# Sum of ReLU over rows: the last two rows closed on two engines, a store moved behind the loads, and the first pieces divided anew

## The chip, the cores and the metric

One core of one Trainium2 chip. The metric is the device time of one execution in microseconds (us). Each run also lists the span that its profile covers; the time is longer than the span, in the kernel before by 1.36 us on average.

## The reference

```python
x: [32, 512, 1024] float32
relu_x = np.maximum(x, 0)
return np.sum(relu_x, axis=-1).astype(np.float32)      # [32, 512]
```

16,384 rows of 1,024 numbers, 67.1 MB in, 64 KB out. The kernel puts 128 rows on the 128 partitions at a time, so there are 128 "rows" per partition.

## The kernel before

The first seven pieces are 16 rows each, in three buffers that take turns. For six of them ScalarE takes the ReLU in a few steps and VectorE sums rows behind it; `ACT_STEPS` and `DVE_STEPS` say how many rows a step has. From the seventh piece on each engine takes whole rows, ReLU and sum in one operation. The end comes in ever smaller loads (8, 4, 2, 1 rows), and the very last row in three parts.

```python
ACT_STEPS = [[7, 9], [7, 9], [4, 5, 7], [4, 5, 7], [4, 5, 7], [3, 4, 5]]
DVE_STEPS = [[7, 9], [7, 4, 5], [4, 5, 7], [4, 5, 7], [4, 5, 7], [3, 4, 5]]
TAIL = [8, 4, 2, 1]
LAST = [512, 224, 288]
# ... cut ...
    parts = [buf[:, tb, r, 0:n0], buf[:, tb, r, n0:n1], last[:, 0 : LAST[2]]]
    for k, (lo, hi) in enumerate([(0, n0), (n0, n1), (n1, D)]):
        sp.dma_start(out=parts[k], in_=xv[-1][:, BIG - 1, lo:hi]).then_inc(
            s_in[NBIG + len(TAIL) + k] if k < 2 else s_part, 16
        )
    sp.wait_ge(s_fact, 1)
    sp.wait_ge(s_fdve, 1)
    sp.dma_start(out=ov[1][:, :], in_=res[:, start[1] : start[2]]).then_inc(s_store, 16)   # bulk store
    sp.wait_ge(s_turn, 1)
    sp.dma_start(out=of[0:P].rearrange(...), in_=turned[0:P:32, 0:32]).then_inc(s_store, 16)
# ... cut: the row before the last is halved, its halves added ...
    n = LAST[2]
    act.wait_ge(s_in[-2], 16)
    on_act(parts[0], last[:, n : n + 1]).then_inc(s_part, 1)
    dve.wait_ge(s_in[-1], 16)
    on_dve(parts[1], last[:, n + 1 : n + 2]).then_inc(s_part, 1)
    dve.wait_ge(s_part, 16 + 2)
    on_dve(last[:, :], res[:, J - 1 : J]).then_inc(s_tdve, 1)      # 288 columns and two partial sums
    sp.wait_ge(s_tdve, 1)
    sp.dma_start(out=ov[-1][:, :], in_=res[:, start[-1] : J]).then_inc(s_out, 16)          # final store
    sp.wait_ge(s_store, 16 * (len(REGIONS) - 1))
    sp.wait_ge(s_out, 16)
```

The last load and the two partial sums lie side by side in `last`, so one operation closes the row (ReLU doesn't change the partial sums, which are never negative).

## Time and profile before

| what | value |
|---|---|
| time, median | 161.09 us (160.91 to 161.38, 3 runs) |
| span of the profiled run | 160.0 us (that run: 161.31 us) |
| DMA share, 9 to 120 us | 1.00, at 433 GB/s |
| VectorE, ScalarE busy | 76%, 63% |
| last load landed | 157.98 us |
| final store issued | 158.49 us |

The DMA stream is full from the start almost to the end (DMA share 0.93 in the first 9 us, 1.00 from there to 120 us, and 1.00 again as the mean of 120 to 150 us). So one reads only the two ends: from the landing of the last loads to the last store. The lines are in the prediction.

### The profile page before, as it was taken

What the parts mean: (1) busy time and instruction counts of PE and PEld (TensorE: products, weight loads), DVE (VectorE), ACT (ScalarE), POOL (GpSimd) and SP (SyncE); (2) the same over time, 40 slices, a digit from 0 to 9 for tenths busy, and PEclk for the clock granted to TensorE, in tenths of its full rate; (3) what the DMA queues carried; (4) which work ended last, traced back from release to release, by engine and by line L of the source; (5) the groups of instructions that cost most, each with busy time, mean ns of one, the idle gap of its engine ahead of it and who ended that gap; (6) DMA issues with size and microseconds to landing.
All of it is one profiled execution on the core that took longest, in us unless ns stands there. A gap on an engine that the chain in (4) does not pass through costs nothing.

```text
span 160.0 us, 150 instructions
## 1 busy us (share of the span) xinstructions
DVE 121.6 (76%) x59; ACT 101.4 (63%) x55; POOL 0.2 (0%) x4
## 2 busy tenths in 40 slices
DVE  0000000999959999999979989699899999598994
ACT  3000059990799708996099942999339980596973
POOL 0000000000000000000000000000000000000000
DMA  9997996996996997997998979969969969999993
GB/s 377 492 399 338 492 524 262 524 524 262 524 508 279 524 475 311 524 442 344 524 410 377 524 344 443 524 295 492 524 295 492 524 262 524 393 393 406 418 387 119
DMA packets 2457, 67.18 MB, mean 420 GB/s; under 512 B 536, under 2 KB 792, under 8 KB 1176
## 3 DMA queue, kind: packets, MB, share of 16 engines
q1 hardware_dynamic: 2456, 67.18, 97.8%
q14 instruction: 1, 0.01, 0.0%
HBM read 67.11 MB, written 0.07 MB: 420 GB/s over the span
## 4 chain that ended last, share of the span: by engine, by line
DMA 68%; ACT 18%; DVE 11%; SPq 1%; issue 0%
DMA buf<-in_x_dram 68%; ACT buf L137 18%; DVE res L152 11%; ACT buf L119 1%; SPq L98 1%; DVE last L122 0%
## 5 line engine op out<-in xcount | busy, mean ns | idle before, releaser
L152 DVE TENSOR_REDUCE res<-buf 128x7 f32<-128x7168 f32 (+4 forms) x17 | 100.1, 5920 | 33.6 <-ACT buf L137 33.6
L137 ACT ACTIVATE buf<-buf 128x7168 f32<-128x7168 f32 (+4 forms) x16 | 80.7, 5099 | 45.9 <-DMA buf<-in_x_dram 45.9
L119 ACT ACTIVATE buf<-buf 128x1024 f32<-128x1024 f32 (+1 forms) x19 | 19.0, 1001 | 9.2 <-DMA buf<-in_x_dram 9.2
L122 DVE TENSOR_SCALAR_CACHE_REDUCE buf<-buf 128x1024 f32<-128x1024 f32 (+2 forms) x19 | 20.8, 1144 | 2.9 <-DMA buf<-in_x_dram 2.7
L119 ACT ACTIVATION_READ_ACCUMULATOR buf<-buf 128x1 f32 x19 | 3.6, 187 | 0.0
L137 ACT ACT_TABLE_LOAD x1 | 1.3, 1283 | 1.3 <-PEq L215 1.3
L122 DVE DVE_READ_ACCUMULATOR buf<-buf 128x1 f32 x19 | 1.6, 82 | 0.0
L122 DVE TENSOR_SCALAR_CACHE_REDUCE last<-last 128x290 f32<-128x290 f32 x1 | 0.5, 455 | 0.2 <-ACT buf L119 0.2
L161 DVE STREAM_TRANSPOSE turned<-res 128x32 f32<-128x32 f32 x1 | 0.2, 211 | 0.0
L185 DVE TENSOR_TENSOR res<-half 128x1 f32<-128x1 f32 x1 | 0.2, 160 | 0.1
L215 POOL MEMSET const-bfloat16-1.0<- 128x1 bf16 x1 | 0.1, 101 | 0.0
L215 POOL MEMSET const-uint8-127<- 128x1 uint8 x1 | 0.1, 101 | 0.0
L215 POOL MEMSET const-float32-0.0<- 128x1 f32 x1 | 0.1, 98 | 0.2 <-issue 0.2
L215 POOL MEMSET const-float32-1.0<- 128x1 f32 x1 | 0.1, 98 | 0.0
L122 DVE DVE_READ_ACCUMULATOR last<-last 128x1 f32 x1 | 0.1, 82 | 0.0
## 6 DMA issues: line engine op xcount, KB each, us to landing
buf<-in_x_dram SPq DMA_DIRECT2D x1, 7680.0 KB, 21.3
buf<-in_x_dram SPq DMA_DIRECT2D x1, 4096.0 KB, 26.7
buf<-in_x_dram SPq DMA_DIRECT2D x1, 2048.0 KB, 31.2
buf<-in_x_dram SPq DMA_DIRECT2D x2, 512.0 KB, 18.8
buf<-in_x_dram SPq DMA_DIRECT2D x1, 1024.0 KB, 33.2
buf<-in_x_dram SPq DMA_DIRECT2D x1, 256.0 KB, 34.4
last<-in_x_dram SPq DMA_DIRECT2D x1, 144.0 KB, 34.3
buf<-in_x_dram SPq DMA_DIRECT2D x1, 112.0 KB, 34.1
```

Of the source, the lines that this page charges most:

```text
L98: sp.dma_start(out=buf[:, tb, r : r + n, :], in_=xv[-1][:, r : r + n, :]).then_inc(s_in[NBIG + i], 16)
L119: return act.activation(t, t, AF.Relu, accum_out=acc)
L122: return dve.tensor_scalar(out=t, in0=t, scalar1=0.0, scalar2=None, op0=ALU.max, op1=ALU.add, accum_out=acc)
L137: act.activation(t, t, AF.Relu).then_inc(s_act, 1)
L152: dve.tensor_reduce(out=res[:, c * BIG + r : c * BIG + r + n], in_=buf[:, c % NB, r : r + n, :], axis=X, op=ALU.add,).then_inc(s_dve, 1)
L161: dve.transpose(out=turned[:, :], in_=res[:, 0:32]).then_inc(s_turn, 1)
L185: dve.tensor_tensor(out=res[:, j0 + r : j0 + r + 1], in0=half[:, 0:1], in1=half[:, 1:2], op=ALU.add)
L215: nc = _bacc.Bacc("TRN2", target_bir_lowering=False, num_devices=1)
```

## The change

Its intent: the last piece becomes a run that crosses the border of the last two rows (112 columns of one, 256 of the other). ScalarE closes the one row and VectorE the other, at the same time. The bulk store of 111 columns of results goes out only when the next to last load has landed; the small store of `turned`, which stood behind it, now goes first. The division of the first pieces is changed as well.

```diff
-ACT_STEPS = [[7, 9], [7, 9], [4, 5, 7], [4, 5, 7], [4, 5, 7], [3, 4, 5]]
-DVE_STEPS = [[7, 9], [7, 4, 5], [4, 5, 7], [4, 5, 7], [4, 5, 7], [3, 4, 5]]
-TAIL = [8, 4, 2, 1]
-LAST = [512, 224, 288]
+ACT_STEPS = [[16], [7, 9], [7, 9], [7, 9], [4, 5, 7], [3, 4, 5]]
+DVE_STEPS = [[4, 5, 7], [7, 4, 5], [7, 4, 5], [7, 4, 5], [4, 5, 7], [3, 4, 5]]
+TAIL = [8, 4, 2]
+CUT = 912
+HEAD = 256
 ... cut ...
+    first, second, third = [(0, CUT), (D + D // 2, 2 * D), (D + HEAD, D + D // 2)]
+    for k, (lo, hi) in enumerate((first, second, third)):
+        sp.dma_start(out=flat[:, lo:hi], in_=rows[:, lo:hi]).then_inc(s_in[NBIG + len(TAIL) + k], 16)
+    sp.dma_start(out=seam[:, 2 : 2 + w + HEAD], in_=rows[:, CUT : D + HEAD]).then_inc(s_seam, 16)
+    ... store of `turned` ...
     sp.wait_ge(s_fact, 1)
     sp.wait_ge(s_fdve, 1)
+    sp.wait_ge(s_in[-1], 16)
     sp.dma_start(out=ov[1][:, :], in_=res[:, start[1] : start[2]]).then_inc(s_store, 16)
 ... cut ...
+    on_act(flat[:, lo : CUT // 2], seam[:, 0:1]).then_inc(s_half, 1)
+    on_dve(flat[:, CUT // 2 : hi], seam[:, 1:2]).then_inc(s_half, 1)
+    ... ScalarE sums `second` (512 columns), VectorE `third` (256) into seam[:, k + HEAD :] ...
+    act.wait_ge(s_seam, 16 + 2)
+    act.wait_ge(s_half, 2)
+    on_act(seam[:, 0:k], res[:, J - 2 : J - 1]).then_inc(s_last, 1)
+    dve.wait_ge(s_seam, 16 + 2)
+    on_dve(seam[:, k : k + HEAD + 2], res[:, J - 1 : J]).then_inc(s_last, 1)
```

More of the change, by code (lines that the diff above doesn't have):

```diff
@@ L36, in bass_relu_sum_kernel @@
     NBIG = len(CHUNKS)
-    assert BIG * NBIG + sum(TAIL) + 1 == J == sum(REGIONS) and sum(LAST) == D
+    assert BIG * NBIG + sum(TAIL) + 2 == J == sum(REGIONS)
     xr = x.rearrange("b s d -> (b s) d")
@@ L48, in bass_relu_sum_kernel @@
     buf = nc.alloc_sbuf_tensor("buf", [P, NB, BIG, D], fp32)
-    last = nc.alloc_sbuf_tensor("last", [P, LAST[2] + 2], fp32)
-    half = nc.alloc_sbuf_tensor("half", [P, 2], fp32)
+    w = D - CUT
+    seam = nc.alloc_sbuf_tensor("seam", [P, 2 + w + HEAD + 2], fp32)
     res = nc.alloc_sbuf_tensor("res", [P, J], fp32)
     turned = nc.alloc_sbuf_tensor("turned", [P, 32], fp32)
-    n_in = NBIG + len(TAIL) + len(LAST) - 1
+    n_in = NBIG + len(TAIL) + 3
     s_in = [nc.alloc_semaphore(f"s_in{i}") for i in range(n_in)]
@@ L60, in bass_relu_sum_kernel @@
     s_half = nc.alloc_semaphore("s_half")
-    s_part = nc.alloc_semaphore("s_part")
-    s_tdve = nc.alloc_semaphore("s_tdve")
+    s_seam = nc.alloc_semaphore("s_seam")
+    s_last = nc.alloc_semaphore("s_last")
     s_turn = nc.alloc_semaphore("s_turn")
@@ L102, in bass_relu_sum_kernel @@
         r += n
-    n0, n1 = LAST[0], LAST[0] + LAST[1]
-    parts = [buf[:, tb, r, 0:n0], buf[:, tb, r, n0:n1], last[:, 0 : LAST[2]]]
-    for k, (lo, hi) in enumerate([(0, n0), (n0, n1), (n1, D)]):
-        sp.dma_start(out=parts[k], in_=xv[-1][:, BIG - 1, lo:hi]).then_inc(
-            s_in[NBIG + len(TAIL) + k] if k < 2 else s_part, 16
-        )
-    sp.wait_ge(s_fact, 1)
-    sp.wait_ge(s_fdve, 1)
-    sp.dma_start(out=ov[1][:, :], in_=res[:, start[1] : start[2]]).then_inc(s_store, 16)
+    rows = xv[-1].rearrange("p j d -> p (j d)")[:, r * D : (r + 2) * D]
+    flat = buf[:, tb, r : r + 2, :].rearrange("p j d -> p (j d)")
+    first, second, third = [(0, CUT), (D + D // 2, 2 * D), (D + HEAD, D + D // 2)]
+    for k, (lo, hi) in enumerate((first, second, third)):
+        sp.dma_start(out=flat[:, lo:hi], in_=rows[:, lo:hi]).then_inc(
+            s_in[NBIG + len(TAIL) + k], 16
+        )
+    sp.dma_start(out=seam[:, 2 : 2 + w + HEAD], in_=rows[:, CUT : D + HEAD]).then_inc(s_seam, 16)
     sp.wait_ge(s_turn, 1)
@@ L115, in bass_relu_sum_kernel @@
     ).then_inc(s_store, 16)
+    sp.wait_ge(s_fact, 1)
+    sp.wait_ge(s_fdve, 1)
+    sp.wait_ge(s_in[-1], 16)
+    sp.dma_start(out=ov[1][:, :], in_=res[:, start[1] : start[2]]).then_inc(s_store, 16)
     def on_act(t, acc):
@@ L171, in bass_relu_sum_kernel @@
                 ins.then_inc(s_fact if i % 2 else s_fdve, 1)
-    for r, n, s in tail[:-1]:
+    for r, n, s in tail:
         act.wait_ge(s, 16)
@@ L177, in bass_relu_sum_kernel @@
             f(buf[:, tb, i, :], res[:, j0 + i : j0 + i + 1])
-    r, _, s = tail[-1]
-    act.wait_ge(s, 16)
-    dve.wait_ge(s, 16)
-    on_act(buf[:, tb, r, 0 : D // 2], half[:, 0:1]).then_inc(s_half, 1)
-    on_dve(buf[:, tb, r, D // 2 : D], half[:, 1:2]).then_inc(s_half, 1)
-    dve.wait_ge(s_half, 2)
-    dve.tensor_tensor(
-        out=res[:, j0 + r : j0 + r + 1], in0=half[:, 0:1], in1=half[:, 1:2], op=ALU.add
-    )
-    n = LAST[2]
+    lo, hi = first
+    act.wait_ge(s_in[-3], 16)
+    dve.wait_ge(s_in[-3], 16)
+    on_act(flat[:, lo : CUT // 2], seam[:, 0:1]).then_inc(s_half, 1)
+    on_dve(flat[:, CUT // 2 : hi], seam[:, 1:2]).then_inc(s_half, 1)
+    k = 2 + w
+    lo, hi = second
     act.wait_ge(s_in[-2], 16)
-    on_act(parts[0], last[:, n : n + 1]).then_inc(s_part, 1)
+    on_act(flat[:, lo:hi], seam[:, k + HEAD : k + HEAD + 1]).then_inc(s_seam, 1)
+    lo, hi = third
     dve.wait_ge(s_in[-1], 16)
-    on_dve(parts[1], last[:, n + 1 : n + 2]).then_inc(s_part, 1)
-    dve.wait_ge(s_part, 16 + 2)
-    on_dve(last[:, :], res[:, J - 1 : J]).then_inc(s_tdve, 1)
-    sp.wait_ge(s_tdve, 1)
+    on_dve(flat[:, lo:hi], seam[:, k + HEAD + 1 : k + HEAD + 2]).then_inc(s_seam, 1)
+    act.wait_ge(s_seam, 16 + 2)
[3 more added lines that the diff above has]
+    on_dve(seam[:, k : k + HEAD + 2], res[:, J - 1 : J]).then_inc(s_last, 1)
+    sp.wait_ge(s_last, 2)
     sp.dma_start(out=ov[-1][:, :], in_=res[:, start[-1] : J]).then_inc(s_out, 16)
```

## The prediction

> **What bounds the kernel now.** I read the page first (shares per engine, then the slices of the DMA row), then the transfer rate in a long stretch, then the chain that ended last, then the instructions of the last four microseconds, and at the end the packets of two short windows.
>
> ```profile
> DVE 121.6 (76%) x59; ACT 101.4 (63%) x55; POOL 0.2 (0%) x4
> ...
> DMA  9997996996996997997998979969969969999993
> ```
>
> ```profile
> 9.00:120.00 111.00, 86.32 (x15) 71.51 (x14) 0.00 (x0) 1.00 1.00 433
> ```
>
> The second fence is one stretch, 9 to 120 us: length, busy DVE, ACT and POOL, clock, DMA share, GB/s. The reader is to see that no engine is full while the transfers are: share 1.00 at 433 GB/s over 111 us. The starts of ScalarE's work on the big pieces in the timeline (41.10, 60.46, 79.80, 99.16, 118.52) are 19.35 us apart, and a piece is 8.39 MB, so 433.5 GB/s. The 67.1 MB need 154.8 us at that rate, out of a span of 160.0. What a change of this kind can touch is therefore only the rest: the start, up to the first bytes, and the end, from the last load to the last store. The end is this:
>
> ```profile
> 122.21 34.19 DMA buf<-in_x_dram
> 156.40 0.02 issue
> 156.42 1.56 ACT buf L119 x4
> 157.98 0.02 issue
> 158.00 0.46 DVE last L122 x2
> ```
>
> ```profile
> 156.95 0.19 ACT L119 ACTIVATION_READ_ACCUMULATOR buf<-buf 128x1 f32 x1
> 157.03 0.08 DVE L122 DVE_READ_ACCUMULATOR buf<-buf 128x1 f32 x1
> 157.08 0.63 ACT L119 ACTIVATE buf<-buf 128x512 f32<-128x512 f32 x1
> 157.17 0.16 DVE L185 TENSOR_TENSOR res<-half 128x1 f32<-128x1 f32 x1
> 157.37 0.39 DVE L122 TENSOR_SCALAR_CACHE_REDUCE buf<-buf 128x224 f32<-128x224 f32 x1
> 157.61 0.19 ACT L119 ACTIVATION_READ_ACCUMULATOR buf<-buf 128x1 f32 x1
> 157.68 0.08 DVE L122 DVE_READ_ACCUMULATOR buf<-buf 128x1 f32 x1
> 158.00 0.46 DVE L122 TENSOR_SCALAR_CACHE_REDUCE last<-last 128x290 f32<-128x290 f32 x1 [0.24 <-ACT buf L119]
> 158.38 0.08 DVE L122 DVE_READ_ACCUMULATOR last<-last 128x1 f32 x1
> 158.49 0.34 SPq L199 DMA_DIRECT2D out_dram<-res  x1
> ```
>
> Columns: start us, length us, engine, line, operation. The chain says that VectorE's closing reduce waited for ScalarE. I don't believe that name. ScalarE's accumulator read ends at 157.80 and VectorE starts at 158.00; where VectorE really waits for ScalarE (157.14 to 157.17, the addition of the halves) the gap is 0.03 us. The same reduce also waits for the last load:
>
> ```profile
> 123.69 0.44 SPq L106 DMA_DIRECT2D last<-in_x_dram  x1
> ```
>
> and the view of that tile gives 34.3 us from its issue to its landing, so 157.99. The last landing is what ends last, and ScalarE follows it by 0.2 us. After it come 0.46 us of VectorE and about 1.5 us of final store (issue at 158.49, landing 1.4 us later).
>
> [...]it is issued at 147.17, yet its small packets are not there then and come with the last loads, where nearly all packets under 512 B lie (these counts also hold a few packets of the completions). First 147.0 to 148.5, then 156.8 to 157.6:
>
> ```profile
> DMA packets 44, 0.64 MB, mean 426 GB/s; under 512 B 5, under 2 KB 5, under 8 KB 5
> ```
> ```profile
> DMA packets 240, 0.14 MB, mean 170 GB/s; under 512 B 170, under 2 KB 240, under 8 KB 240
> ```
>
> [...]the store's runs are 444 B (111 x 4). [...]the trace shows the second as an 82 ns read on VectorE and a 187 ns read on ScalarE.
>
> **The change part by part.**
> 1. *First pieces.* ScalarE takes piece 0 in one step of 16 rows. From 7,168 to 9,216 elements it goes from 6.17 to 7.87 us, 0.83 ns each, so 16,384 need 13.8 us: 21.75 + 13.8 = 35.6, where VectorE now starts (27.96 before). A piece in steps of 4, 5 and 7 costs VectorE 17.30 us (65.07 to 82.37), and the new order leaves it no wait between pieces: it finishes pieces 0 to 4 at 52.9, 70.2, 87.7 (with 0.2 of transpose), 105.0 and 122.3. These release the loads of pieces 3 to 6 and the tail. The loads ahead of them end at 60.4, 79.8, 99.1, 118.5 and 137.9. The smallest margin is 7.5 us: no bubble, 0 us. Piece 5 costs two rows alone (2.28) and 13.07: done at 137.65, just before piece 6 lands at 137.87, with another 0.5 us of VectorE idle time before the next landing. 0 us.
> 2. *Bytes of the end.* The last two rows were loads of 1024, 512, 224 and 288 columns and are now 912, 512, 256 and 368: same 2,048 columns, same four packets per partition. Last byte unmoved. The first load is 448 B per partition shorter: it lands some 0.13 us earlier, 156.27. The second lands near 156.90, the third, 32 columns more than before, near 157.24.
> 3. *ScalarE.* 1045 ns for 1,024 columns and 630 for 512 give 0.81 ns a column: 456 take 0.585, 156.27 to 156.86. It waits for the second load, runs 512 columns from 156.92 and has read its sum by 157.64 (before: 157.80).
> 4. *VectorE.* 685 ns for 512 and 386 for 224 give 1.04 ns a column: 456 take 0.63, done by 156.95; 256 take 0.42 from the third landing, sum read by 157.70. The addition (0.16 us) goes; it was hidden beside ScalarE.
> 5. *Closing.* Both engines now wait for the last load and for each other, then ScalarE closes 114 columns (0.31, with its read 0.41 us) while VectorE closes 258 (0.42, with its read 0.45 to 0.49; before 0.46 for 290). VectorE still ends last, 0.03 us sooner than before for its fewer columns.
> 6. *Bulk store late.* It now waits for the third load, so it is issued near 157.26, for 0.35 us, over long before the closing. From the final store (issue 158.49, first bytes seen in the window from 159.2 on) I estimate its packets at about 158.1, after all loads, and its landing near 158.9, before the final store's near 159.7. Nothing waits for it. What it gives is that the last load's stragglers no longer share the engines' final half microsecond with 128 packets of 444 B. Other loads of the end landed about 0.35 us after their last bytes (rate falls to nothing around 157.36, landing 157.99 is 0.6 after): if the store caused this excess, the landing comes about 0.25 earlier, 157.73.
>
> Sum: with the landing at 157.73 both engines are ready at 157.70, the closing ends near 158.22 instead of 158.46: 0.24 us gained. With the landing unmoved: 0.0 to 0.03. Weighted evenly and rounded up a little, since such a variant would hardly be kept for nothing: 0.2 us off 161.09, **160.87 us**.
>
> **The rivals.**
> (a) *The last landing is late for its own reasons.* For it: [...]the byte count is unchanged. Then the kernel stays at 161.05 to 161.1 and the chain names the load openly. Against: the earlier loads land with less lag.
> (b) *A new wait replaces the old.* Two engines must both finish and each needs the other's partial sum; a late ScalarE would hold VectorE too. It would need ScalarE over 0.1 us later than in step 3; its second load would have to land after 157.0. Time 161.1 to 161.2.
> (c) *The stream is starved early.* VectorE releases buffers up to 7.4 us later than before. Against: margins of 7.5 us and more. If wrong, several us, 163 or so; improbable.
> (d) *The late store delays the end*, being the last to land or holding the issuing queue. Against: 0.7 us of margin by the estimate in step 6. If wrong, 161.3.
>
> **Range and chances.** The runs before spread by 0.47 us (160.91 to 161.38), more than the effect. Two thirds for a gain of 0.1 to 0.4, a quarter for nothing, the rest for a small loss: 160.45 to 161.25. Over 2% would be 3.2 us; the whole end after the last load is about 2.7 us, so it can't be gained there: 0.005. Slower by that much needs (c): 0.005.
>
> **What would show it.** Step 1: VectorE without gaps from 35.6 to about 137.6, DMA share at 1.00 in the middle, pieces landing every 19.35 us. Steps 3 and 4: partial sums at about 157.65 and 157.70. Step 5: both closings start together, within 0.05 us of the last landing. Step 6: packets under 512 B gone from 156.8 to 157.6 save for completions, last landing near 157.7. The prediction is wrong if the DMA rate dips in the middle, if the closings start at 158.0 again, or if the final wait ends on the bulk store.

Its sum comes to 0.2 us off, 160.87 us; that the store causes the late landing, on which its 0.24 us case rests, was the author's assumption. The stream counts as full by the DMA share of 1.00 in its second fence. The store that "is issued at 147.17" is the bulk store. In the trace of the kernel before, its 128 packets of 444 B, 25 ns each, run from 156.84 to 157.54, and the 128 packets of the last load from 156.46 to 157.36. Which of the 16 engines carry them was not shown. The "completions" are packets of 4 B: the trace has 277 of them, as many as there are semaphore increments by DMA. The "second" of 82 and 187 ns is the read of the accumulator, a line of its own behind each reduce in the timeline.

## The result, and the profile after

The changed kernel takes 160.81 us median (160.72 to 161.02, 6 runs), the kernel before 161.06 us (160.91 to 161.38, 6 runs). The ratio is 0.9985, with a 95% interval of 0.9972 to 0.9998. A ratio is the mean time of one kernel's fast runs over that of the other's in the same rounds, so it isn't quite the ratio of these medians. By the limit of 2% the two are the same; the small gain is just clear of noise, and it came again in a second set (160.81 against 160.97, ratio 0.9983, interval 0.9969 to 0.9998).

The stretch from 9 to 120 us of the changed kernel, in the columns of the prediction's fence:

```profile
9.00:120.00 111.00, 84.47 (x16) 71.38 (x11) 0.00 (x0) 1.00 1.00 433
```

The stream is untouched: same share, same rate. The chain that ended last, in order of time (start us, length us, what):

```profile
35.50 34.59 DVE res L160 x6
...
124.39 32.60 DMA buf<-in_x_dram
156.99 0.02 issue
157.01 0.44 DVE buf L130 x2
157.45 0.02 issue
157.47 0.43 DVE seam L130 x2
```

VectorE starts at 35.50 and runs without a gap, as the prediction's first step has it. The chain has grown a long VectorE part (55% of the span, 11% before). That isn't a new bound: the loads it releases stand in the queue before their turn comes, the first of them 7.4 us (issued at 52.86, the load ahead of it landed at 60.29), the last ones over 30 us. The end of the timeline:

```profile
157.01 0.42 DVE L130 TENSOR_SCALAR_CACHE_REDUCE buf<-buf 128x256 f32<-128x256 f32 x1 [0.40 <-DMA buf<-in_x_dram]
157.08 0.34 SPq L123 DMA_DIRECT2D out_dram<-res  x1
157.19 0.19 ACT L127 ACTIVATION_READ_ACCUMULATOR buf<-buf 128x1 f32 x1
157.36 0.08 DVE L130 DVE_READ_ACCUMULATOR buf<-buf 128x1 f32 x1
157.47 0.30 ACT L127 ACTIVATE seam<-seam 128x114 f32<-128x114 f32 x1
157.47 0.42 DVE L130 TENSOR_SCALAR_CACHE_REDUCE seam<-seam 128x258 f32<-128x258 f32 x1
157.68 0.19 ACT L127 ACTIVATION_READ_ACCUMULATOR seam<-seam 128x1 f32 x1
157.82 0.08 DVE L130 DVE_READ_ACCUMULATOR seam<-seam 128x1 f32 x1
157.93 0.34 SPq L207 DMA_DIRECT2D out_dram<-res  x1
```

ScalarE's sum is read at 157.37, VectorE's at 157.44, and the last load lands at 157.44. All three meet, and both closings start at 157.47. They end at 157.86 and 157.90. The packets from 156.8 to 157.6, where 170 of under 512 B lay before:

```profile
DMA packets 15, 0.01 MB, mean 15 GB/s; under 512 B 7, under 2 KB 15, under 8 KB 15
```

The bulk store is gone from there. The final wait of the issuing queue is still on the final store (1.1 us), not on the bulk store, whose last increment comes at 159.05, 0.30 us before that of the final store.

From these two profiles alone one would say that the final store goes out 0.56 us earlier (158.49 to 157.93). That is more than twice what the medians show. The profiled run of before was one of its slower ones (161.31), so the question is which part of the 0.56 us is the change. Of it, 0.13 us is there already when the load of two rows lands (154.94 and 154.81), with nothing changed up to then that bears on it. Experiments had to sort the rest.

### The profile page after: what moved, and what is told of

It is laid out like the page before. It is cut to its first block, busy times and chain, and to the rows that moved or that the text cites. A ratio compares the mean times of both kernels' runs of the same rounds, so it can differ in the third digit from the quotient of the medians.

```text
span 159.4 us, 150 instructions
## 1 busy us (share of the span) xinstructions
DVE 120.6 (76%) x59; ACT 101.5 (64%) x54; POOL 0.2 (0%) x4
## 4 chain that ended last, share of the span: by engine, by line
DVE 55%; DMA 34%; ACT 9%; SPq 2%; issue 0%
DVE res L160 54%; DMA buf<-in_x_dram 34%; ACT buf L145 9%; SPq L101 1%; SPq L112 1%; DVE buf L130 0%; DVE seam L130 0%; SPq L91 0%; DVE turned L169 0%
## 5 line engine op out<-in xcount | busy, mean ns | idle before, releaser
L160 DVE TENSOR_REDUCE res<-buf 128x4 f32<-128x4096 f32 (+3 forms) x18 | 99.4, 5596 | 35.5 <-ACT buf L145 35.5
L145 ACT ACTIVATE buf<-buf 128x7168 f32<-128x7168 f32 (+5 forms) x13 | 80.4, 6233 | 46.1 <-DMA buf<-in_x_dram 46.1
L127 ACT ACTIVATE buf<-buf 128x1024 f32<-128x1024 f32 (+2 forms) x19 | 19.0, 999 | 8.9 <-DMA buf<-in_x_dram 8.9
```

What stands on the lines that cost most here:

```text
L127: return act.activation(t, t, AF.Relu, accum_out=acc)
L145: act.activation(t, t, AF.Relu).then_inc(s_act, 1)
L160: dve.tensor_reduce(out=res[:, c * BIG + r : c * BIG + r + n], in_=buf[:, c % NB, r : r + n, :], axis=X, op=ALU.add,).then_inc(s_dve, 1)
```

## The experiments

Theory S: the early bulk store, whose 128 packets run beside those of the last load (156.84 to 157.54 us, the load's 156.46 to 157.36), delays the last increments of the last load; moving it is the gain. Rival C: the late landing was an accident of one execution. Rival R: the cut of the last rows is the gain. Rival E: the division of the first pieces is the gain. All kernels gave correct results, and each had its profile from one of its runs. In the first two groups the kernel before ran 11 times, in the third 9 times, on the same chip.

"Spacing" below is the time from the landing of the next to last load to that of the last, read from the semaphore increments in the trace. The last load has 288 columns in the old end and 368 in the new.

| run | end, bulk store | spacing, us | median time, us | ratio (95% interval) | span, outside it (mean, us) |
|---|---|---|---|---|---|
| before, first profile | old, early | 0.63 | | | |
| e1_before_again | old, early | 0.36 | 161.00 | 0.9999 (0.9987 to 1.0011) | 159.66, 1.38 |
| e2_store_late_only | old, late | 0.34 | 161.00 | 0.9995 (0.9983 to 1.0007) | 159.62, 1.37 |
| e3_steps_only | old, early | 0.36 | 161.42 | 1.0023 (1.0010 to 1.0037) | 159.87, 1.57 |
| e4_seam_only | new, early | 0.80 | 161.21 | 1.0004 (0.9992 to 1.0017) | 159.63, 1.53 |
| changed, first profile | new, late | 0.45 | 160.81 | 0.9985 (0.9972 to 0.9998) | 159.48, 1.36 |
| f1_after_store_early | new, early | 0.80 | 160.97 | 0.9993 (0.9976 to 1.0009) | 159.62, 1.37 |
| f2_after_old_steps | new, late | 0.45 | 161.04 | 0.9998 (0.9982 to 1.0014) | 159.48, 1.57 |
| f3_store_in_four_early | old, early, 4 stores | 0.64 | 161.07 | 1.0000 (0.9983 to 1.0016) | 159.73, 1.37 |
| f4_after_again | new, late | 0.46 | 160.81 | 0.9983 (0.9969 to 0.9998) | 159.48, 1.35 |
| g1_before_more_act | old, early | 0.37 | 161.33 | 1.0022 (1.0009 to 1.0035) | 159.98, 1.35 |
| g2_after_old_dve_steps | new, late | 0.47 | 161.34 | 1.0025 (1.0012 to 1.0037) | 159.52, 1.85 |
| g3_steps_only_again | old, early | 0.70 | 161.34 | 1.0015 (1.0001 to 1.0028) | 159.68, 1.56 |
| g4_store_on_act_queue | new, in mid-stream | 0.48 | 161.16 | 1.0013 (1.0001 to 1.0026) | 159.62, 1.56 |

Spans are given to 0.1 us a run; the table has their means. The 31 runs of the kernel before that stood beside these twelve have a mean span of 159.68.

**The kernel before, again.** No edit.

> The kernel before, unchanged, as the measure of chance. Both theories: ratio to the kernel before 1.000 within 0.0015. Its profile decides what is systematic: theory S (the early bulk store delays the last load's stragglers) expects the last load of 288 columns to land about 0.6 us after the 224 columns before it again (0.64 in the first profile, 0.37 by its bytes). Rival C (the late landing was an accident of that one execution) expects about 0.4. Of the row of 1,024 columns, which took 1.46 us where 1.22 follow from its bytes, S says nothing; if it is systematic, it is 1.4 again, if accident, about 1.25.

Time equal, spacing 0.36: the late landing did not come again. Neither did the slow row of 1,024 columns (1.28 us after the two rows, where the first profile had 1.45). Its end:

```profile
157.42 0.18 ACT L119 ACTIVATION_READ_ACCUMULATOR buf<-buf 128x1 f32 x1
157.51 0.08 DVE L122 DVE_READ_ACCUMULATOR buf<-buf 128x1 f32 x1
157.64 0.46 DVE L122 TENSOR_SCALAR_CACHE_REDUCE last<-last 128x290 f32<-128x290 f32 x1
...
158.13 0.34 SPq L199 DMA_DIRECT2D out_dram<-res  x1
```

Here the last load landed at 157.54 and ScalarE's sum came at 157.61, so ScalarE does hold the closing in an execution that isn't late. One profile had shown only one of two cases.

**The bulk store late, with the old end and the old division.** The store of `turned` (512 B) moves ahead of it, as in the changed kernel, so this run doesn't move the bulk store quite alone.

```diff
+    sp.wait_ge(s_turn, 1)   # store of `turned` first
     ...
     sp.wait_ge(s_fdve, 1)
+    sp.wait_ge(s_in[-1], 16)
     sp.dma_start(out=ov[1][:, :], ...)
```

> The kernel before with the bulk store alone moved behind the next to last load. Theory S: the last load lands some 0.4 us after the one before it, the closing reduce starts near 157.8 and is then bound by ScalarE's sum (157.80), time 0.15 to 0.2 us under the kernel before (ratio near 0.999). Rival C: landing and time unchanged (ratio 1.000 within 0.0007).

The spacing is 0.34, but the median does not move (161.00, as the kernel before again), and its mean, 160.99, lies 0.06 us under the mean of e1, inside the noise. Its runs are close together (160.88 to 161.06), while those of before reach 161.35. ScalarE's sum holds the closing here too, so moving the store is worth nothing in an execution whose last load is on time anyway (three of the six profiles with the old end and the early store). S, as a theory of the median, misses.

**The new division of the first pieces, and nothing else.** The first two lines of the change's diff.

> The kernel before with the new division of the first pieces alone. Both S and the prediction's step 1: no effect, ratio 1.000 within 0.001, pieces landing every 19.35 us, VectorE without gaps from 35.6 to about 137.6. Rival E (the early pieces carry the gain, through the transfers issued later or fewer instructions): ratio 0.9985, the pieces of the middle landing earlier by 0.1 to 0.2 us in relation to the first one.

A miss for everyone: 0.4 us slower. Its spacing is on time, but its pieces landed 19.36 to 19.47 us apart, and its time outside the span is 1.57, not 1.36. It was run again below.

**The new last rows, with the old division and the early store.**

```diff
 (all of the change but:)
+ACT_STEPS, DVE_STEPS as before
+    bulk store at its early place
```

> The new last two rows alone: old division of the first pieces, bulk store issued early as before. Theory S: the last load still lands late (some 0.65 us or more after the third, where 0.45 follow from its bytes), so the closings start late and the time is within 0.05 us of the kernel before, at most 0.1 under it. Rival R (the rows' cut carries the gain: a shorter first load, no 4,096 B packets, two engines closing): ratio 0.9985 to 0.999, the last load landing 0.45 us after the third.

Spacing 0.80 where 0.45 belong to 368 columns: late, as S has it, and no gain. R alone misses. Again 1.53 us lie outside the span.

**The changed kernel with the early store.**

```diff
-    sp.wait_ge(s_in[-1], 16)     # and the bulk store ahead of the store of `turned`
```

> The changed kernel with the bulk store put back to its early place (the loads and the arithmetic as in the changed kernel). Theory S: the last load lands 0.65 us or more after the third instead of 0.45, the closings start 0.2 us later, time 0.15 to 0.25 us over the changed kernel, so ratio to the kernel before 0.9995 to 1.000. Rival R (the cut of the rows carries the gain): ratio 0.9985 as the changed kernel.

Spacing 0.80 again. The lines show what that costs, since all else is ready at 157.48:

```profile
157.23 0.19 ACT L126 ACTIVATION_READ_ACCUMULATOR buf<-buf 128x1 f32 x1
157.40 0.08 DVE L129 DVE_READ_ACCUMULATOR buf<-buf 128x1 f32 x1
157.86 0.30 ACT L126 ACTIVATE seam<-seam 128x114 f32<-128x114 f32 x1 [0.44 <-DVE buf L129]
157.86 0.42 DVE L129 TENSOR_SCALAR_CACHE_REDUCE seam<-seam 128x258 f32<-128x258 f32 x1 [0.38 <-DVE buf L129]
```

Both engines idle some 0.4 us. The view names VectorE as the releaser, which had been done for 0.38 us; it is the load, landed at 157.84. The six runs fall in two groups: 160.76, 160.78, 160.84 and 161.10, 161.15, 161.29. The first group is as fast as the changed kernel, the second 0.4 us slower, about as much as the spacing is longer (0.35) in the profile, which is of one of the second group (161.15). The spans fall in the same two groups (159.4 to 159.5 and 159.7 to 159.9). This fits a lateness that comes and goes from run to run; only the one run has a profile, so for the others it is an inference.

**The changed kernel with the old division of the first pieces.** The first two lines of the diff undone.

> The changed kernel with the old division of the first pieces. S and R: the same as the changed kernel, ratio to the kernel before near 0.9985. Rival E (the division of the first pieces carries the gain): ratio 1.000 within 0.0005.

By the time, this is the number of rival E (0.9998), and S and R miss: without the new division the gain is gone. But e3 had E miss by 0.4 us, so the division doesn't carry a gain of its own. The mean span is that of the changed kernel to the hundredth, 159.48, yet the time is 161.04. All of the difference, 0.2 us, lies outside the span (1.57 against 1.35). In a window from 159 us on, the two instruction packets of this profile come after the span's end (159.4):

```profile
q14 instruction: 2, 0.02, 1.3%
```

while the page, which counts the span, has no such line for it, and has one packet for the kernel before.

**The early store in four.** Columns 0 to 28, 28 to 56, 56 to 84 and 84 to 111, in the old end.

```diff
-    sp.dma_start(out=ov[1][:, :], in_=res[:, start[1] : start[2]]).then_inc(s_store, 16)
+    for a, b in ((0, 28), (28, 56), (56, 84), (84, 111)):
+        sp.dma_start(out=ov[1][:, a:b], in_=res[:, start[1] + a : start[1] + b]).then_inc(s_store, 16)
```

> The suspected cost enlarged: the kernel before with its early bulk store cut into four of 28, 28, 28 and 27 columns, so 512 packets of about 112 B in the place of 128 of 444 B[...]. Theory S: the stragglers of the last load are disturbed for longer, it lands 0.7 us or more after the 224 columns before it, time 0.1 to 0.5 us over the kernel before. Rival C: the last load lands some 0.4 to 0.6 us after and the time is within 0.05 us, unless the stores themselves end after the final store.

Spacing 0.64: late, but no later than the 0.63 and 0.70 of one store, with four times the packets. The time is that of before. In these profiles the lateness did not grow with the number of packets.

**The changed kernel, again.** No edit.

> The changed kernel again, for comparison on the same chip and a second profile. Ratio to the kernel before 0.9985 within 0.001; the last load lands 0.45 us after the third; both closings start together within 0.05 us of that landing.

As expected in all points: 0.9983, spacing 0.46, both closings at 157.53 after a landing at 157.50.

**More ScalarE instructions in the kernel before.** After f2 a new theory F was formed: that with a longer ScalarE program the two instruction packets come after the end of the span, as in the profiles of e4 and f2, and the time grows.

```diff
-ACT_STEPS = [[7, 9], [7, 9], [4, 5, 7], ...
+ACT_STEPS = [[4, 3, 4, 5], [4, 3, 4, 5], [4, 5, 7], ...
```

> New theory F: [...](in the two kernels with the new last rows and the old first pieces, two instruction packets lie after the span; in all others one lies within it). Here the kernel before with ScalarE's first two pieces cut in four steps each, four ScalarE instructions more, all far from the end. F: no instruction packet within the span, two after it, time 0.1 to 0.15 us over the kernel before with the same span. Rival G (what was seen belongs to the new last rows, or to chance): one packet within the span, time unchanged within 0.05 us.

F misses as it was put: the time outside the span is 1.35, and both packets lie within it. But the kernel is 0.4 us slower all the same, and within the span, though the last load landed at 157.43 and the final store was issued at 158.02, earlier than in the profile of before. The DMA view of this run:

```profile
q14 instruction: 2, 0.02, 0.0%
...
out_dram<-res SPq DMA_DIRECT2D x1, 8.0 KB, 1.8
```

The final store took 1.8 us to land, where the kernel before, the changed kernel, f2 and f4 show 1.4. Fifteen of its 16 increments came by 159.46, the last at 159.85; one of the two instruction packets ran from 159.30 to 159.60. That this packet held up the last increment is an inference from these times, not shown by an experiment of its own. It can't be the packet's presence alone: in the changed kernel a packet starts just as long after the issue of the final store (1.28 us), in e1 1.27 us after, and there no increment is late. What only g1 has is a first packet from 158.65 to 158.97.

**The changed kernel with VectorE's old division only.** The second line of the diff undone.

> The changed kernel with the old division on VectorE and the new one on ScalarE (three ScalarE instructions fewer than with the old one). F: one instruction packet within the span, time as the changed kernel, 160.8 (ratio to the kernel before 0.9985). Rival D (VectorE's new order of steps, which leaves no gaps, is what gives the last 0.2 us): 161.0, as with both old divisions.

F misses again, and so does rival D: the mean span is 159.52, as in the changed kernel, but 1.85 us lie outside it, and the time is 161.34.

**The new division alone, again.** As e3.

> The kernel before with the new division of the first pieces alone, a second time, since the first run gave 161.42[...]. If that was chance of that load or moment: 161.05 within 0.1, pieces landing every 19.35 us. If the division itself slows the stream in this kernel: 161.4 again with 19.42 to 19.47 us between landings.

On another chip the pieces land every 19.35 us. The slow pieces of e3 (19.36 to 19.47 us apart) did not come again there, but 1.56 us outside the span did. Spacing 0.70, so late.

**The bulk store from ScalarE's queue, in mid-stream.**

```diff
-    (bulk store on SP)
+    act.wait_ge(s_fact, 1)
+    act.wait_ge(s_fdve, 1)
+    act.dma_start(out=ov[1][:, :], in_=res[:, start[1] : start[2]]).then_inc(s_store, 16)
     for r, n, s in tail:
```

> The changed kernel with the bulk store issued by ScalarE as soon as its results are there (near 147.1),[...] so that its 128 packets run in the middle of the loads and neither behind the last of them nor after them. Theory S (the lateness comes from stores running beside the last load's stragglers): the last load lands 0.45 us after the third, as in the changed kernel. The stream itself pays for the bytes: 128 packets of about 25 ns over 16 engines are 0.2 us, so landings from there on are 0.1 to 0.2 later and the time is 160.9 to 161.0. Rival H (any early store delays the end's small loads): 0.65 us or more between third and last, 161.1 or more.

The issue, and the packets between 152 and 154 us:

```profile
147.03 0.38 ACTq L178 DMA_DIRECT2D out_dram<-res  x1
```
```profile
DMA packets 190, 0.85 MB, mean 426 GB/s; under 512 B 90, under 2 KB 90, under 8 KB 90
```

The store's packets (90 of queue q10 in this window, where the loads are 100 of q1) run among the loads, and the last load is on time (0.48). The stream pays for them: the load of two rows lands 0.11 us later than in the changed kernel (154.92 against 154.81; counted from the landing of the seventh piece 17.21 us, against 17.10 to 17.13 in the changed kernel, f2, f4 and g2). The mean span is 159.62, 0.14 above the changed kernel's, as estimated; another 0.2 us lie outside the span. No version beats the changed kernel.

**Taken together.** With the early store in the loads' own queue the last load was late in five of eight profiles, by 0.28 to 0.35 us over the on-time spacing of the same size. With the store late or in mid-stream it was late in none of six. That the place of the stores makes the difference is thus likely. f1 and the changed kernel differ in it alone, and their profiles show it (0.80 against 0.45 and 0.46); in time the difference, 0.15 us between the means of f1 and f4, isn't clear of the noise of six runs, and one run of the changed kernel has a span of 159.7 as well. Not tested: the store of `turned` always moved with the bulk store. In the six profiles it is issued by 128 us, in the eight after 147 us, so its part can't be told apart. Nor does g4 tell the queue from the time, as it changes both.

What is late can be read from the traces, which keep the 16 increments of a load one by one:

| the last load | nine profiles on time | five late ones |
|---|---|---|
| from the end of its last packet to its landing, us | 0.39 to 0.47 | 0.62 to 0.83 |
| widest gap between two increments, us | 0.05 to 0.12 | 0.27 to 0.43 |

In the late ones that gap stands before the last increment (in f1 before the last three). So what comes late is not the load's data but one to three of its 16 increments; in the first profile alone the last packet, too, ended some 0.2 us late. Why one increment waits in some executions is open.

In executions that are on time, the span from the landing of the two rows to the issue of the final store is 3.21 to 3.23 us in the old end (e1, e2, e3, g1) and 3.10 to 3.18 in the new (changed, f2, f4, g2, g4). The cut of the rows is worth 0.03 to 0.13 us, about 0.1: the closing waits no more for ScalarE (0.10 us from landing to closing in e1, 0.03 in the changed kernel), and the closing has 32 columns fewer.

The time outside the span has means of 1.35 to 1.38 us in six programs here, 1.53 to 1.57 in four (e3 and g3 are one program) and 1.85 in one (g2). In the profiles of e4, f2, g2 and g4 an instruction packet starts over 1 us after the end of the span (160.71 to 161.21), in those of before, changed, e3, g1 and g3 none does. So such a packet goes with the longer time in four programs of five: e3 and g3, with 1.57 and 1.56 us outside, have none. What sets the time outside stays open; the number of ScalarE instructions alone does not (g1: four more, and 1.35).

## Why the prediction was right

The time, 160.81, lies 0.06 us from the predicted 160.87 and well inside the range. Its points:

- *The bound.* Right: DMA share and rate in the middle are the same to the digit, and only the end moved.
- *First pieces, 0 us.* Right within the span: VectorE started at 35.50 (35.6 predicted) and the pieces landed every 19.35 us. What the step left out is the time outside the span. There the division is worth about 0.2 us beside the new end (changed kernel against f2) and costs as much beside the old one (e3, g3).
- *Bytes of the end.* The last load landed 2.63 us after the two rows, and 2.58 to 2.63 in e1, e2 and e3 with the old end: the last byte unmoved, right. The landings themselves came 0.25 to 0.34 us earlier than predicted, because I took the slow start and the slow row of one profile for the rule.
- *ScalarE and VectorE.* From second landing to ScalarE's sum 0.75 us (0.74 predicted), from third landing to VectorE's sum 0.45 (0.46 predicted).
- *Closing.* Both started together, 0.03 us after the last landing; VectorE took 0.43 us, predicted 0.45 to 0.49.
- *Late store.* The excess of the last landing was put at 0.25 us; where it occurs it is 0.28 to 0.35. It doesn't always occur.
- *The sum.* This is the part that was off in size. "With the landing unmoved: 0.0 to 0.03" was too small: the cut of the rows gives about 0.1 us in executions that are on time. The case with the landing at 157.73, "0.24 us gained", takes the lateness as constant, whereas e1 and e2 show that moving the store alone does nothing for the median of the old end. The two errors lie in opposite directions. Of the rivals, (a) was half true, as chance from run to run, and (b), (c) and (d) did not come; but for (d) the margin was 0.30 us, not 0.7.
- *Luck.* The number is nearer than its working. The 0.2 us came from weighing two cases evenly and rounding up because such a variant "would hardly be kept for nothing", which is no reading of a trace. And the time outside the span, of which the prediction says nothing, could have undone the gain: with the old division (f2) it does.

So the gain of some 0.2 us (mean span 159.68 to 159.48, time outside it 1.36 in both) is both parts: the cut, which helps every execution by about 0.1 us, and the late store, which takes away the late ones. Each alone leaves the other limit standing: e2 is held by ScalarE's sum, f1 by late landings. The share of the cut is shown in the spans, that of the store is likely. The division adds nothing in the span, but beside this end it keeps the time outside at 1.36 us; why, no run shows.

## What to carry to other kernels

When an end is tuned to tenths of a microsecond, take several profiles of the same kernel before you believe a wait in one: here one profile showed the load as the last to come, and the next showed ScalarE. Try stores that nobody waits for behind the last loads, but early enough to land before the final store (here by 0.30 us). Compare spans as well as times: here other steps in the first pieces, which left the mean span at 159.48 (f2) and 159.52 (g2), moved the time by 0.2 and 0.5 us outside it.
